# Longer weight runs with a new DMA model in the planner, a gain folded into weights, and three small steps moved to ScalarE in a decoder step on eight cores

## The chip, the cores and the metric

The kernel runs as one program on the 8 cores of one Trainium2 chip, each core on its own share of the batch. The time is device microseconds (us) of the slowest core. A program on all eight cores has a second, slower state in some executions: one die of four cores, or both, then shows a lower granted TensorE clock and the time is some per cent longer.

In the profile PE is TensorE, PEld its weight load, DVE VectorE, ACT ScalarE, POOL GpSimd and SP SyncE. A line such as `AR<-w_out` names the destination and the source of an operation. `pb` is a bank of PSUM and `AR` is the large working area in SBUF. Nearly every operation is emitted by one helper, so all carry the line number L252 and are told apart by their tiles and shapes. In the code cuts `ts`, `tt`, `stt`, `scan`, `act` and `cp` are helpers that record one elementwise operation each, and `dma` records a load. `...` marks what is left out, and comments are mine.

## The reference, cut to what matters

The step is one decoder layer for 2048 prompt tokens and 128 sample tokens per core. A mixer (one input projection, two head groups, one output projection) is followed by a squared-ReLU MLP and by a gated per-layer embedding.

```python
z = rmsnorm(h, norm_mix) @ w_in
u, vg, q, k, vm, o, zi, zf = jnp.split(z, SPLITS, axis=-1)
u  = gelu(u);  vg = layernorm(gelu(vg), gm_ln_g, gm_ln_b)         # head group A
y_gm = _gmlp_mix(u, vg, gm_ws, gm_bs, gm_len)
ig = zi + ml_b_i;  lf = log_sigmoid(zf + ml_b_f)                  # the gate rows, head group B
hm, state = _mlstm(q, k, vm, ig, lf, state, ml_len)
hm = rmsnorm(hm.reshape(B, T, ML_HEADS, ML_HEAD_DIM), ml_norm)    # the gain that is folded
y_ml = sigmoid(o) * hm
h = h + concat([y_gm, y_ml]) @ w_out
h = h + square(relu(rmsnorm(h, norm_ffn) @ w_up)) @ w_down        # the MLP
...                                                               # gated embedding, final norm
```

The tiles of 128 tokens are worked off in two passes: 8 prompt tiles and the sample tile first, then the other 8 prompt tiles. Each pass is a mixer and then an MLP. The weights are loaded again in the second pass.

Of the kernel before, what the change touches and what calls it, by code (L numbers as in the profile page):

```python
# [312 lines left out]
class Op:  # L313
    __slots__ = ("eng", "dma", "calls", "reads", "writes", "cost", "nbytes", "idx", "rank", "preds", "succs", "npred",
                 "pts", "tset", "fin", "tready", "after", "tok", "tag", "__dict__")
# [9 lines left out]
class Plan:  # L325
# [66 lines left out]
    def schedule(self, caps):  # L392
# [28 lines left out]
        while len(order) < n:  # L421
# [48 lines left out]
            if o.dma:  # L470
                free[e] = s + o.cost
                d0 = max(free[e] + 1.0, dma_free)
                dma_free = d0 + o.nbytes / 290e3
                o.fin = dma_free + 1.2
            else:
                o.fin = free[e] = s + o.cost
                if e == "act" and o.tset is not None:
                    tabs = (SETS[o.tset] & tabs) or SETS[o.tset]
# [32 lines left out]
def build():  # L511
# [27 lines left out]
    P = Plan()  # L539
    from contextlib import ExitStack  # L540
    with ExitStack() as st:
# [78 lines left out]
        def dma(out, in_, eng="sp", after=(), **kw):  # L620
            nb = 4 * _nelem(out) * list(out.ap)[0][1]
            return P.add(eng, (out, in_, kw), [in_], [out], 0.9 if eng == "pool" else 0.06, dma=True, nbytes=nb,
                         after=after)
# [87 lines left out]
        WIN = [WA.bf(8 * 512, k8(8)) for _ in range(6)]  # L711
# [7 lines left out]
        COLS = dict(u=0, v=512, q=1024, k=1536, m=2048, o=2560)  # L719
        WSLOT = dict(u=0, v=1, o=2, q=3, k=4, m=5)  # L720
        WORDER = ("u", "v", "o", "q", "k", "m")
# [57 lines left out]
        def load_win(names, **kw):  # L779
            v = w_in.rearrange("(k p) n -> p k n", p=128)  # L780
            for nm in names:
                dma(WIN[WSLOT[nm]], v[:, :, COLS[nm]:COLS[nm] + 512], eng="pool", **kw)
# [7 lines left out]
        load_win("u")  # L790
# [72 lines left out]
        def stage_P(grp):  # L863
# [6 lines left out]
            def feat(nm, fin):  # L870
                w = WIN[WSLOT[nm]]
                for hp in range(2):
                    p = ps("P")
                    for hh in range(2):
                        h = hp * 2 + hh
                        mm(p[:, hh * n:(hh + 1) * n],
                           [(w[:, kc, h * 128:(h + 1) * 128], at[:, kc, 0:n]) for kc in range(8)])
                    fin(p[:, 0:2 * n].rearrange("p (h t) -> p h t", h=2), slice(hp * 2, hp * 2 + 2))

            def tokm(nm, j):  # L880
                w = WIN[WSLOT[nm]]
                p = ps("P")
                mm(p, [(at[:, kc, j * 128:(j + 1) * 128], w[:, kc, :]) for kc in range(8)])
                return p
# [3 lines left out]
            for j, t in enumerate(grp):  # L888
                vn = VN[t["n"] % 2]
                act(vn, tokm("v", j), AF.Gelu_apprx_tanh)  # L890
                st6, mv, tm, rs = small(t["n"], 4, 6), small(t["n"], 10, 2), small(t["n"], 12, 1), small(t["n"], 13, 1)
                dve("bn_stats", st6, vn)
                dve("bn_aggr", mv, st6)
                rstd(rs, tm, mv[:, 1:2], 1.0, EPS)
                ts("dve", vn, vn, mv[:, 0:1], ALU.subtract, rs, ALU.mult)
                tt("pool", XH[t["n"] % 3], vn, GROW[:], ALU.mult)
                if t["ty"] == 1 or t["i"] == NPT - 1:
                    brow = SQ.rearrange("p h t -> p (h t)")
                    dma(brow, lnb.partition_broadcast(128), after=marks)
                    tt("pool", vn, vn, GROW[:], ALU.mult)  # L900
                    tt("pool", vn, vn, brow, ALU.add)
                    dma(o_Vs if t["ty"] == 1 else o_Vp, vn)
# [3 lines left out]
            for h in range(4):  # L906
                ts("dve", SGT[d2][:, h, 0:n], SGT[d2][:, h, 0:n], 1.0, ALU.add, GN[:, G_MLG + h:G_MLG + h + 1], ALU.mult)
            feat("q", lambda p, hs: cp("act", QT[d2][:, hs, 0:n], p))
            feat("k", lambda p, hs: act(KT[d2][:, hs, 0:n], p, AF.Copy, scale=QK_SCALE))
            for j, t in enumerate(grp):  # L910
                cp("act", VAUG[t["n"] % 4][:, :, 0:128], tokm("m", j).rearrange("p (h d) -> p h d", h=4))
            return pg, marks

        def stage_G(grp, pg):
# [11 lines left out]
            ts("dve", aa, pg[0:4, 0:n], GBI[0:4, 0:1], ALU.add)  # L926
# [28 lines left out]
            ts("dve", r3[0:4, 0:n], RR, -1.0, ALU.mult)  # L955
# [45 lines left out]
        def stage_M(grp, gs):  # L1001
# [3 lines left out]
            for j, t in enumerate(grp):  # L1005
# [80 lines left out]
                tt("dve", yt[:, 4:8, :], py[:, 0:512].rearrange("p (h t) -> p h t", h=4), SGT[d2][:, :, tk], ALU.mult)  # L1086
# [27 lines left out]
        def load_q(qd):  # L1114
            wu, wd = WU[qd % 2], WD[qd % 2]
            w_up_v = w_up.rearrange("(k p) n -> p k n", p=128)
            for hf in range(2):
                c0 = qd * 1024 + hf * 512
                dma(wu[:, :, hf * 512:(hf + 1) * 512], w_up_v[:, :, c0:c0 + 512], eng="pool")
# [55 lines left out]
        for si, sg in enumerate(SGS):  # L1175
# [3 lines left out]
            if si > 0:  # L1179
                load_win("uvoq")  # L1180
                P.tag = "vaug"
                for v_ in VAUG:
                    memset("pool", v_[:, :, 128:129], 1.0)
            for gi_, grp in enumerate(groups):
# [8 lines left out]
                if si == 0 and gi_ == 0:  # L1193
                    load_win("v", after=nops[:1])
# [4 lines left out]
                    load_win("o", after=nops[1:])  # L1199
                    nops = stage_N(groups[1], 1)  # L1200
                    load_win("qkm", after=nops)
                    dma(WOUT, w_out.rearrange("(k p) n -> p k n", p=128), eng="pool", after=nops)
                elif gi_ == 0:
                    load_win("km")
                    dma(WOUT, w_out.rearrange("(k p) n -> p k n", p=128), eng="pool")
# [139 lines left out]
```

## The kernel before: the parts that the change and the argument touch

The code that builds the kernel records all operations with what they depend on, and a **planner** then puts them into one fixed order for each engine. On the chip each engine works through its own list in that order. The planner is a list scheduler: again and again it takes the operation that can start first by its own cost model. Ties within 0.02 us go to the one written earlier.

```python
CROSS, SAME = 0.22, 0.06
TABLE = 1.3                                   # us, charged for a ScalarE function-table load
# Plan.schedule, shortened
for o in ready[e]:
    s = max(free[e], o.tready)
    if e == "pe":
        ...                                   # PSUM banks
    elif e == "act" and o.tset is not None and not (SETS[o.tset] & tabs):
        s += TABLE                            # Exp, Ln, Tanh, Gelu; a copy (Copy, Identity) has no tset
    cand.append((s, o))
s0 = min(c[0] for c in cand) + 0.02
best[e] = min((c for c in cand if c[0] <= s0), key=lambda c: c[1].rank)
...
if o.dma:                                     # the model of DMA: one queue, in order, 290 bytes per ns
    free[e] = s + o.cost
    d0 = max(free[e] + 1.0, dma_free)
    dma_free = d0 + o.nbytes / 290e3
    o.fin = dma_free + 1.2
```

What must stay in order comes from `_link`. For a PSUM tile, uses by the same engine form a run without order inside it, and a run waits for all of the run before it. So two reads of one PSUM tile by **different** engines are ordered, and two reads by the **same** engine are not.

```python
if r and r[-1][0] == o.eng and r[-1][1] == w and (o.eng == "pe" or not w):
    r[-1][2].append(o.idx)                    # same engine, same kind: joins the run
else:
    r.append((o.eng, w, [o.idx]))
if len(r) > 1:
    P.update(r[-2][2])                        # the whole run before must be done
```

The loads at the start and the steps that the change moves:

```python
def load_win(names, **kw):                    # six blocks of 512 columns of w_in, 2 KB runs, on POOL's queue
    v = w_in.rearrange("(k p) n -> p k n", p=128)
    for nm in names:
        dma(WIN[WSLOT[nm]], v[:, :, COLS[nm]:COLS[nm] + 512], eng="pool", **kw)

def consts_b(af):                             # issued after all weights of the mixer, w_out last
    dma(OH[:], coh, eng="pool", after=af)     # one-hot table: brings the gate rows to all partitions by matmul
    dma(MSK[:], cmask, after=af)              # no eng: SyncE's queue
    ...

# stage_P
ts("dve", vn, vn, mv[:, 0:1], ALU.subtract, rs, ALU.mult)                    # layernorm scaling
...
for h in range(4):                            # (1 + tanh) * gain, the gain of ml_norm
    ts("dve", SGT[d2][:, h, 0:n], SGT[d2][:, h, 0:n], 1.0, ALU.add, GN[:, G_MLG + h:G_MLG + h + 1], ALU.mult)

# stage_G: pg is one PSUM tile with both gate rows
act(L, pg[32:36, 0:n], AF.Exp, bias=GBI[32:36, 1:2], scale=-1.0)             # ScalarE
act(L, L, AF.Ln, bias=1.0)                                                   # ScalarE
ts("dve", aa, pg[0:4, 0:n], GBI[0:4, 0:1], ALU.add)                          # VectorE
scan(NB, L, ZROW[0:4, 0:n], 0.0, ALU.add, ALU.max)                           # VectorE, needs Ln
...
ts("dve", r3[0:4, 0:n], RR, -1.0, ALU.mult)

# stage_M
mmx([(pc[:, h, :], OH[:, h, :], r3[:, tk], True, True) for h in range(4)])   # "the OH matmul", first of them at 90 us
...
tt("dve", yt[:, 4:8, :], py[...], SGT[d2][:, :, tk], ALU.mult)               # gating
```

## Time and profile before

| | before |
|---|---|
| time, median of the three runs before the change | 1023.42 us (1022.73 to 1027.23) |
| TensorE busy on the slowest core | 895.8 of 1020.3 us (88%) |
| VectorE, ScalarE busy | 581.2 us, 391.8 us |
| first OH matmul starts | 90.8 us |
| software DMA queue (POOL's), share of 16 engines | 40.9% |

The page of the kernel before starts with busy time by engine. Its second part cuts the span into 40 slices of about 25.5 us, with one digit each for the busy tenths; PEclk is the granted TensorE clock in tenths.

```profile
PE 895.8 (88%) x5807; PEld 539.0 (53%) x5875; DVE 581.2 (57%) x1118; ACT 391.8 (38%) x711; POOL 264.4 (26%) x370
...
PE   2578898937999999999997678998899999999994
PEclk9798899967999999999999889999999999999997
```

TensorE is the bound, and its row of digits says where it is not full: the first three slices, slice 9 with a 3 (the sample tile), and slices 22 to 25 with 6 to 8 (the turn to the second pass). The view of waits names what TensorE waited for (total us, times, longest). Here `sC` is the state of the samples, `pp` and `psm` are the embedding inputs of the prompt and the samples, and `wgate` (tile WGT) holds the weights of the gate rows. The two longest entries, waits for ScalarE (31.8) and VectorE (29.6), are left out in this cut:

```profile
...
PE pb L252 <- DMA AR<-sC: 15.7, 1, 15.7
PE pb L252 <- DMA AR<-w_in: 10.7, 2, 6.7
...
PE pb L252 <- DMA AR<-pp: 3.6, 1, 3.6
```

OH is the last load that POOL issues at the start (its next one follows at 53.9 us), as the timeline (start, length, engine) and then the DMA view (KB each, us from issue to landing) show:

```profile
27.14 0.90 POOL L276 DMA_DIRECT2D AR<-w_out  x1
28.00 0.59 POOL L276 DMA_DIRECT2D OH<-coh  x1
...
90.83 0.61 PE L252 MATMUL pb<-R_0,OH 128*128 128x128 bf16 x8
```

```profile
OH<-coh POOLq DMA_DIRECT2D x1, 128.0 KB, 59.0
```

A load of 128 KB took 59 us to land, because it stood behind megabytes of weights on the same queue. The first OH matmul comes 4 us after the landing. The windows view (busy us and count for each engine in each stretch, then clock and DMA share) shows stretches at work:

```profile
core 2: us, PE busy (x) PEld busy (x) DVE busy (x) ACT busy (x) POOL busy (x), PEclk, DMA share, GB/s
60.00:80.00 20.00, 14.64 (x116) 10.70 (x114) 9.66 (x24) 8.46 (x17) 4.50 (x5) 0.91 1.10 179
640.00:660.00 20.00, 18.23 (x147) 11.84 (x150) 18.36 (x42) 12.19 (x21) 10.18 (x14) 1.00 0.00 1
660.00:680.00 20.00, 19.74 (x162) 14.69 (x163) 18.07 (x46) 12.06 (x22) 7.16 (x9) 1.00 0.00 1
```

In the second mixer (640 to 680 us) TensorE and VectorE are both nearly full.

The groups that the change means to remove or alter (busy us and mean ns, then idle before them):

```profile
L252 DVE TENSOR_SCALAR AR<-AR,GN 128x256 bf16<-128x256 bf16 x32 | 12.6, 434 | 9.9 <-ACT AR L252 9.7
...
L252 DVE TENSOR_SCALAR AR<-AR,SMALL 128x512 f32<-128x512 f32 x17 | 10.6, 626 | 6.6 <-POOL SMALL L252 6.4
...
L252 DVE TENSOR_TENSOR AR<-pb,AR 128x512 bf16<-128x512 bf16 x17 | 7.0, 414 | 0.1
```

These are the gate gain, the layernorm scaling and the gating.

### The profile page before, as it was taken

The numbers are of one execution on the slowest core, as the hardware profiler recorded it, in microseconds if no ns is written. First come the engines' busy times: TensorE is split into PE (matmuls) and PEld (weight loads), VectorE is DVE, ScalarE is ACT, GpSimd is POOL, SyncE is SP. The second block draws the span as 40 slices with busy tenths as digits, with TensorE's granted clock in tenths as the row PEclk, the third lists the DMA queues.
The fourth block names the chain that finished last, engine by engine and source line by source line (L and its number), as shares of the span: only waits on it lengthen the run. The fifth ranks groups of instructions, "written<-read, shape, count | busy, mean of one in ns | idle before, by whom it ended". The sixth has DMA issues, their size and how long they took to land.

```text
span 1020.3 us, 17111 instructions; the slowest of 8 cores (1003.6 to 1020.3 us)
## 1 busy us (share of the span) xinstructions
PE 895.8 (88%) x5807; PEld 539.0 (53%) x5875; DVE 581.2 (57%) x1118; ACT 391.8 (38%) x711; POOL 264.4 (26%) x370
## 2 busy tenths in 40 slices
PE   2578898937999999999997678998899999999994
PEld 2465476624455555555553267576656555565542
DVE  2354878445656774444665537988864444445664
ACT  4245356425311121114544547655532112124543
POOL 3233345443202220011232323545520001001211
PEclk9798899967999999999999889999999999999997
DMA  9993010996677768065249400003999909000111
GB/s 166 183 172 45 12 45 6 109 146 97 104 142 136 177 161 133 1 86 88 86 105 203 121 22 2 1 2 51 138 144 162 161 2 155 11 1 4 68 45 62
DMA packets 80689, 90.59 MB, mean 89 GB/s; under 512 B 13656, under 2 KB 62044, under 8 KB 80604
## 3 DMA queue, kind: packets, MB, share of 16 engines
q0 software_dynamic: 54224, 59.18, 40.9%
q1 hardware_dynamic: 26380, 30.32, 9.8%
q8 instruction: 48, 0.79, 0.3%
q14 instruction: 37, 0.30, 0.1%
HBM read 134.74 MB, written 13.93 MB: 146 GB/s over the span
## 4 chain that ended last, share of the span: by engine, by line
PE 75%; DMA 9%; DVE 6%; issue 5%; ACT 3%; POOL 2%; DVEq 0%; SPq 0%; POOLq 0%; ACTq 0%
PE pb L252 75%; DVE AR L252 3%; DMA AR<-sC 3%; DMA AR<-w_in 3%; DMA AR<-pp 2%; ACT AR L252 2%; POOL SMALL L252 1%; DMA H<-xp 1%; DVE H L252 1%; DVE SMALL L252 1%; DVE ROWX L252 1%; ACT L252 1%; POOL AR L252 0%; DVE ROWR L252 0%; POOL CST L252 0%
## 5 line engine op out<-in xcount | busy, mean ns | idle before, releaser
L252 PE MATMUL pb<-AR 128*128 128x512 bf16 (+4 forms) x4856 | 838.0, 331 | 62.3 <-DVE AR L252 20.9
L252 PEld LDWEIGHTS pb<-AR 128*128 128x128 bf16 x4924 | 470.8, 100 | 393.8 <-issue 86.3
L252 ACT ACTIVATE AR<-pb 128x384 f32<-128x384 f32 (+5 forms) x349 | 175.5, 513 | 476.0 <-PE pb L252 387.7
L252 DVE TENSOR_TENSOR H<-H,pb 128x512 f32<-128x512 f32 x170 | 116.4, 685 | 136.5 <-PE pb L252 136.3
L252 DVE TENSOR_TENSOR AR<-AR 128x384 bf16<-128x384 f32 (+2 forms) x209 | 122.8, 589 | 109.1 <-ACT AR L252 108.3
L252 ACT ACTIVATE AR<-H 128x1024 bf16<-128x1024 f32 x68 | 71.7, 1054 | 54.4 <-PE pb L252 26.9
L252 PE MATMUL pb<-IDB,AR 128*128 128x128 bf16 x578 | 53.5, 237 | 42.6 <-ACT AR L252 28.7
L252 POOL TENSOR_SCALAR SMALL<-SMALL 128x1 f32<-128x1 f32 x85 | 26.3, 310 | 245.4 <-ACT AR L252 201.9
L252 DVE TENSOR_TENSOR AR<-pb,GN 128x1024 bf16<-128x1024 bf16 x51 | 61.6, 1218 | 36.4 <-PE pb L252 36.4
L252 POOL TENSOR_TENSOR SMALL<-SMALL,NEGH 128x1 f32<-128x1 f32 (+1 forms) x102 | 69.3, 681 | 49.8 <-DVE SMALL L252 29.6
L252 PEld LDWEIGHTS pb<-IDB,AR 128*128 128x128 bf16 x578 | 43.0, 107 | 57.7 <-issue 48.9
L252 ACT ACTIVATE AR<-H,SMALL 128x1024 bf16<-128x1024 f32 x51 | 58.1, 1145 | 35.3 <-POOL SMALL L252 34.9
L276 POOL DMA_DIRECT2D AR<-w_up x16 | 15.0, 935 | 132.7 <-PE pb L252 132.3
L252 DVE TENSOR_TENSOR AR<-pb,AR 128x512 f32<-128x512 f32 (+3 forms) x86 | 43.7, 523 | 9.4 <-ACT AR L252 8.4
L252 ACT ACT_TABLE_LOAD x29 | 37.2, 1283 | 16.1 <-PE pb L252 10.2
L252 DVE SCALAR_TENSOR_TENSOR AR<-AR,pb 128x512 f32<-128x512 f32 x34 | 23.2, 684 | 29.6 <-PE pb L252 20.8
L252 ACT ACTIVATE AR<-AR 128x512 f32<-128x512 f32 x34 | 21.3, 629 | 23.8 <-DVE AR L252 17.2
L252 POOL TENSOR_TENSOR AR<-AR,GROW 128x512 bf16<-128x512 f32 (+1 forms) x19 | 25.5, 1341 | 16.5 <-PE pb L252 8.5
L276 POOL DMA_DIRECT2D AR<-w_in x12 | 11.0, 920 | 68.3 <-PE pb L252 64.3
L252 DVE SCALAR_TENSOR_TENSOR AR<-H,SMALL,AR 128x1024 f32<-128x1024 f32 x17 | 22.9, 1346 | 9.1 <-POOL SMALL L252 8.7
L252 ACT ACTIVATE AR<-pb,GSM 128x129 f32<-128x129 f32 x68 | 20.7, 366 | 13.7 <-PE pb L252 13.5
L276 POOL DMA_DIRECT2D AR<-w_down x16 | 12.2, 765 | 51.4 <-PE pb L252 51.3
(101 smaller groups left out, 434.7 us busy)
## 6 DMA issues: line engine op xcount, KB each, us to landing
AR<-w_up POOLq DMA_DIRECT2D x16, 1024.0 KB, 16.0
AR<-w_down POOLq DMA_DIRECT2D x16, 1024.0 KB, 18.9
AR<-w_in POOLq DMA_DIRECT2D x12, 1024.0 KB, 17.5
H<-xp SPq DMA_DIRECT2D x16, 512.0 KB, 4.6
y_p<-AR SPq DMA_DIRECT2D x16, 512.0 KB, 2.9
AR<-w_out POOLq DMA_DIRECT2D x2, 2048.0 KB, 41.8
AR<-sC SPq DMA_DIRECT2D x8, 512.0 KB, 5.0
AR<-w_pg POOLq DMA_DIRECT2D x2, 2048.0 KB, 27.4
```

Source lines behind the costliest of these rows:

```text
L252: ins = getattr(e, name)(**kw)
L276: lambda e, out=out, in_=in_, sem=sem, kw=kw: e.dma_start(out=out, in_=in_, **kw).then_inc(sem, 16))
```

## The change

The intent has three parts. Weights are to be read in runs of 4 KB instead of 2 KB, for fewer and larger packets. The gain of ml_norm is to be multiplied once into the rows of w_out, and no longer into each tile's gate. Work is to move from VectorE (57% busy) to ScalarE (38%). With the first part comes a new model of DMA in the planner.

```diff
             if o.dma:
                 free[e] = s + o.cost
-                d0 = max(free[e] + 1.0, dma_free)
-                dma_free = d0 + o.nbytes / 290e3
-                o.fin = dma_free + 1.2
+                took = o.nbytes / o.rate
+                if o.nbytes < 2e6:                        # "small" loads do not queue
+                    o.fin = free[e] + 2.2 + took * (2 if dma_free > free[e] + 1 else 1)
+                    dma_free = max(dma_free, free[e] + 1) + took
+                else:
+                    dma_free = max(free[e] + 1.5, dma_free) + took
+                    o.fin = dma_free + 1.2
...
+            o.rate = (320e3 if run >= 4096 else 265e3 if run >= 2048 else 180e3) * (1.0 if eng == "pool" else 1.1)
...
-        WIN = [WA.bf(8 * 512, k8(8)) for _ in range(6)]
+        WPAIR = [WA.bf(8 * 1024, k8(8)) for _ in range(3)]   # u|v, m|o, q|k
...
+        def load_wout(af):
+            dma(WOUT, w_out.rearrange("(k p) n -> p k n", p=128), eng="pool", after=af)
+            for h in range(4):
+                ts("dve", WOUT[:, 4 + h, :], WOUT[:, 4 + h, :], GN[:, G_MLG + h:G_MLG + h + 1], ALU.mult)
...
-                ts("dve", vn, vn, mv[:, 0:1], ALU.subtract, rs, ALU.mult)
+                nm = small(t["n"], 14, 1)
+                stt("dve", nm, mv[:, 0:1], -1.0, rs, ALU.mult, ALU.mult)
+                act(vn, vn, AF.Identity, bias=nm, scale=rs)
...
-            for h in range(4):
-                ts("dve", SGT[d2][:, h, 0:n], SGT[d2][:, h, 0:n], 1.0, ALU.add, GN[...], ALU.mult)
...                                                          # m is now projected before q and k
-            ts("dve", aa, pg[0:4, 0:n], GBI[0:4, 0:1], ALU.add)
+            act(aa, pg[0:4, 0:n], AF.Identity, bias=GBI[0:4, 0:1])
...
-            ts("dve", r3[0:4, 0:n], RR, -1.0, ALU.mult)
+            act(r3[0:4, 0:n], RR, AF.Copy, scale=-1.0)
...
-                tt("dve", yt[:, 4:8, :], py[...], SGT[d2][:, :, tk], ALU.mult)
+                stt("dve", yt[:, 4:8, :], SGT[d2][:, :, tk], 1.0, py[...], ALU.add, ALU.mult)
...
-            for hf in range(2):                              # w_up: two loads of 512 columns
-                dma(wu[:, :, hf * 512:(hf + 1) * 512], w_up_v[:, :, c0:c0 + 512], eng="pool")
+            dma(wu, w_up_v[:, :, qd * 1024:(qd + 1) * 1024], eng="pool")
...
-                load_win("uvoq")
+                load_win(["uv", "mo"])
...
-                    load_win("qkm", after=nops)
-                    dma(WOUT, ..., eng="pool", after=nops)
+                    load_win(["qk"], after=nops)
+                    load_wout(nops)
```

At the start u and v are still loaded one by one, and o, m, q, k in pairs.

More of the change, by code (lines that the diff above doesn't have):

```diff
@@ L314 @@
     __slots__ = ("eng", "dma", "calls", "reads", "writes", "cost", "nbytes", "idx", "rank", "preds", "succs", "npred",
-                 "pts", "tset", "fin", "tready", "after", "tok", "tag", "__dict__")
+                 "pts", "tset", "fin", "tready", "after", "tok", "tag", "rate", "__dict__")
 SETS = {"gelu": frozenset(("g",)), "tanh": frozenset(("g", "e")), "exp": frozenset(("e", "l")),
@@ L621, in dma @@
             nb = 4 * _nelem(out) * list(out.ap)[0][1]
-            return P.add(eng, (out, in_, kw), [in_], [out], 0.9 if eng == "pool" else 0.06, dma=True, nbytes=nb,
-                         after=after)
+            run = min(list(out.ap)[-1][1], list(in_.ap)[-1][1]) * 4
+            o = P.add(eng, (out, in_, kw), [in_], [out], 0.9 if eng == "pool" else 0.06, dma=True, nbytes=nb,
+                      after=after)
+            o.rate = (320e3 if run >= 4096 else 265e3 if run >= 2048 else 180e3) * (1.0 if eng == "pool" else 1.1)
+            return o
         def mmx(items):
@@ L718, in build, with win @@
         WD[1] = WB.bf(8 * 1024, k8(8))
-        COLS = dict(u=0, v=512, q=1024, k=1536, m=2048, o=2560)
-        WSLOT = dict(u=0, v=1, o=2, q=3, k=4, m=5)
-        WORDER = ("u", "v", "o", "q", "k", "m")
+        COLS = dict(u=0, v=512, q=1024, k=1536, m=2048, o=2560, uv=0, qk=1024, mo=2048)
+        WLOC = dict(u=(0, 0), v=(0, 512), m=(1, 0), o=(1, 512), q=(2, 0), k=(2, 512), uv=(0, 0), mo=(1, 0), qk=(2, 0))
+        def win(nm):
+            i_, o_ = WLOC[nm]
+            return WPAIR[i_][:, :, o_:o_ + 512 * len(nm)]
         AB = [LOW.bf(DM) for _ in range(2)]
@@ L781, in load_win @@
             for nm in names:
-                dma(WIN[WSLOT[nm]], v[:, :, COLS[nm]:COLS[nm] + 512], eng="pool", **kw)
+                dma(win(nm), v[:, :, COLS[nm]:COLS[nm] + 512 * len(nm)], eng="pool", **kw)
+        def load_wout(af):
+            dma(WOUT, w_out.rearrange("(k p) n -> p k n", p=128), eng="pool", after=af)
+            for h in range(4):
+                ts("dve", WOUT[:, 4 + h, :], WOUT[:, 4 + h, :], GN[:, G_MLG + h:G_MLG + h + 1], ALU.mult)
         P.tag = "start"
@@ L789, in build @@
         memset("pool", NEGH[:], -0.5)
-        load_win("u")
+        load_win(["u"])
         cp("dve", IDB[:], IDF[:])
@@ L870, in feat @@
             def feat(nm, fin):
-                w = WIN[WSLOT[nm]]
+                w = win(nm)
                 for hp in range(2):
@@ L880, in tokm @@
             def tokm(nm, j):
-                w = WIN[WSLOT[nm]]
+                w = win(nm)
                 p = ps("P")
@@ L905, in stage_P @@
             feat("o", lambda p, hs: act(SGT[d2][:, hs, 0:n], p, AF.Tanh, scale=0.5))
-            for h in range(4):
-                ts("dve", SGT[d2][:, h, 0:n], SGT[d2][:, h, 0:n], 1.0, ALU.add, GN[:, G_MLG + h:G_MLG + h + 1], ALU.mult)
+            for j, t in enumerate(grp):
+                cp("act", VAUG[t["n"] % 4][:, :, 0:128], tokm("m", j).rearrange("p (h d) -> p h d", h=4))
             feat("q", lambda p, hs: cp("act", QT[d2][:, hs, 0:n], p))
             feat("k", lambda p, hs: act(KT[d2][:, hs, 0:n], p, AF.Copy, scale=QK_SCALE))
-            for j, t in enumerate(grp):
-                cp("act", VAUG[t["n"] % 4][:, :, 0:128], tokm("m", j).rearrange("p (h d) -> p h d", h=4))
             return pg, marks
@@ L1085, in stage_M @@
                 trs([(py[:, h * 128:(h + 1) * 128], yml[:, h, :], IDB[:]) for h in range(4)])
-                tt("dve", yt[:, 4:8, :], py[:, 0:512].rearrange("p (h t) -> p h t", h=4), SGT[d2][:, :, tk], ALU.mult)
+                stt("dve", yt[:, 4:8, :], SGT[d2][:, :, tk], 1.0, py[:, 0:512].rearrange("p (h t) -> p h t", h=4),
+                    ALU.add, ALU.mult)
                 for nn in range(2):
@@ L1116, in load_q @@
             w_up_v = w_up.rearrange("(k p) n -> p k n", p=128)
-            for hf in range(2):
-                c0 = qd * 1024 + hf * 512
-                dma(wu[:, :, hf * 512:(hf + 1) * 512], w_up_v[:, :, c0:c0 + 512], eng="pool")
+            dma(wu, w_up_v[:, :, qd * 1024:(qd + 1) * 1024], eng="pool")
             for hf in range(2):
@@ L1193, in build @@
                 if si == 0 and gi_ == 0:
-                    load_win("v", after=nops[:1])
+                    load_win(["v"], after=nops[:1])
                     for t in groups[1]:
@@ L1198, in build @@
                     dma(WGT[:], wgate.rearrange("(k p) n -> p k n", p=128), eng="pool", after=nops[1:])
-                    load_win("o", after=nops[1:])
+                    load_win(["mo"], after=nops[1:])
                     nops = stage_N(groups[1], 1)
-                    load_win("qkm", after=nops)
-                    dma(WOUT, w_out.rearrange("(k p) n -> p k n", p=128), eng="pool", after=nops)
+                    load_win(["qk"], after=nops)
+                    load_wout(nops)
                 elif gi_ == 0:
-                    load_win("km")
-                    dma(WOUT, w_out.rearrange("(k p) n -> p k n", p=128), eng="pool")
+                    load_win(["qk"])
+                    load_wout(())
                 P.tag = f"A{si}P{gi_}"
```

## The prediction

> What bounds the kernel now. The page gives TensorE 88% busy (896 of 1020 us), VectorE 57%, ScalarE 38%. In the windows view the two MLP stretches are saturated (262-530 us: 265 of 268 busy; 740-980 likewise). The ~124 idle us of TensorE sit in six places: the start, 0-87 us (53 busy of 87); the first mixer part, 87-190 (90 of 103); the sample tile, 190-219 (13 of 29, one wait of 15.7 us for the state load AR<-sC); 219-262 (32 of 43); the turn from the first pass to the second, 530-600 (50 of 70, with a 3.6 us wait for AR<-pp); the second mixer part, 600-740 (128 of 140); and the tail.
>
> DMA. Start: the 16 DMA engines are above 100% busy from 20 to 80 us. The POOL queue delivers in order u, v, wgate, o, q, k, m, w_out and last the one-hot table OH, which lands at 87 us; the first OH matmul starts at 90.8. Packets of 1024 B (a 2 KB run cast to bf16) take 98 ns median, 117 mean; 2048 B packets (w_down, w_out, 4 KB runs) 173 median, 200-210 mean: 11-15% less per byte. The Trainium skill, "DMA: Bandwidth & Descriptors", section "Why small descriptors are slow (HBM only)", names a fixed cost per packet; these two durations agree. Over the kernel 26,600 packets of 1024 B become 13,300 of 2048 B: about 33 us of 16-engine time, software queue 40.9% to about 38%. On the critical path lie only: m,o,q,k before OH, 4 x 1024 x (118-105 ns)/16 = 3-5 us; w_up ahead of sC, about 2 us; k,m ahead of pp at the turn, 2-3 us. Against it: o waits for its whole 4 MB pair (one block is 7.7 us); and the w_up load waits for both u and v to be free (2.7 us later here). The planner no longer queues small loads behind large ones, although sC and pp really waited 23-28 us; it may place their matmuls too early.
>
> VectorE. Removed, by groups: gate gain TENSOR_SCALAR 15.1 us, layernorm scale 10.6, gate rows aa and r3 6.7. Added, estimated: nm 17 x 0.17 = 2.9, w_out scaling 8 x 0.42 = 3.3, and the gating op, 0.41 us as a TENSOR_TENSOR in bf16, as SCALAR_TENSOR_TENSOR probably 0.68 (the rate that op shows here): +4.6. Net about -21 (581 to 560). ScalarE gains 17 x 0.63 + 18 x 0.42 = +18 (392 to 410). VectorE is near full only at 100-120 and 620-680 us (18 of 20): I expect 2-5 us of TensorE idle back in the mixer parts; aa and r3 on ScalarE lengthen the gate chain by two engine crossings.
>
> Sum: start -4, sample tile and turn -3, mixer -4, order changes +-6: about 1012 us. Interval 998 to 1023. Chances: faster by over 2% 0.16, within 2% 0.82, slower 0.02.
>
> Right if: queue near 38%; OH lands near 82-84 us; VectorE falls by about 20 us, ScalarE rises by about 18, table loads stay at 29 or fewer; TensorE's busy time is unchanged and idle falls by about 11 us, mostly before 90 us and in the mixer parts.
>
> Wrong if: the static order moves sC or pp matmuls so that these waits grow (slower), or the sC wait or the turn, 16 and 20 idle us, largely vanishes by a better order (faster); if HBM, shared by cores, not packet cost, limits the start, 4 KB runs bring nothing.

## More of the kernel before

TensorE works 14.6 of 20 us while it has no OH.

The timeline of the first gate rows of the second pass:

```profile
601.38 1.28 ACT L252 ACT_TABLE_LOAD   x1 [0.26 <-PE pb L252]
602.68 0.47 ACT L252 ACTIVATE ROWL<-pb,GBI 4x256 f32<-4x256 f32 x1
603.25 0.47 DVE L252 TENSOR_SCALAR ROWX<-pb,GBI 4x256 f32<-4x256 f32 x1 [1.05 <-ACT ROWL L252]
...
619.23 1.28 ACT L252 ACT_TABLE_LOAD   x1
620.52 0.41 ACT L252 ACTIVATE ROWL<-ROWL 4x256 f32<-4x256 f32 x1
...
621.04 0.68 DVE L252 TENSOR_TENSOR_SCAN ROWN<-ROWL,ZROW 4x256 f32<-4x256 f32 x1 [3.94 <-ACT ROWL L252]
```

The first ACTIVATE is Exp, the second is Ln, ROWX is the row `aa`, and the scan can start 18.4 us after Exp. Note the releaser of `aa`: it waited for ScalarE's Exp, although it does not need its result. That is the order edge of `_link`.

## The result, and the profile after

| | before | after |
|---|---|---|
| median of 4 fast runs | 1024.8 us (1022.73 to 1027.23) | 1069.66 us (1066.66 to 1071.08) |
| ratio, with 95% interval | | 1.0433 (1.0397 to 1.0469) |
| TensorE busy / idle on the slowest core | 895.8 / 124.5 us | 901.7 / 166.6 us |
| VectorE, ScalarE busy | 581.2, 391.8 us | 564.5, 406.8 us |
| mean granted clock, die medians | 0.956, 0.957 | 0.936, 0.938 |

The kernel became 4.3% slower, where about 1012 us (998 to 1023) had been predicted. A ratio in this document is the mean time of one kernel's fast runs over that of the other's fast runs of the same rounds, so it is not quite the ratio of the medians quoted beside it. Results were correct in every run.

The engines did about what was predicted of them: VectorE fell by 16.7 us and ScalarE rose by 15.0. The loss is TensorE's idle time, and the page shows it mainly in two places. (The trace of the slowest core before lacks 68 of the 5875 matmuls, so its busy time is read a little low.)

```profile
PE 901.7 (84%) x5875; PEld 539.6 (51%) x5875; DVE 564.5 (53%) x1072; ACT 406.8 (38%) x743; POOL 253.5 (24%) x357
...
PE   3503999867979899999996789789699999999994
PEclk9756999998989999999998889899889999999997
```

The third slice (53 to 80 us) went from 7 to 0. And slices 26 and 27 (about 670 to 720 us, in the second mixer) are 7 and 8, where the kernel before has two 9s. TensorE's waits:

```profile
PE pb L252 <- DMA OH<-coh: 36.3, 1, 36.3
...
PE pb L252 <- DMA WGT<-wgate: 14.8, 1, 14.8
PE pb L252 <- DMA AR<-sC: 11.0, 3, 4.9
PE pb L252 <- DMA AR<-psm: 10.6, 1, 10.6
```

The waits for OH, wgate and psm did not exist before, and all are for small loads; the one for sC did. Over the eight cores the wait for OH is 28.3 to 36.3 us, with a median of 31.3. Did OH land later? Timeline and DMA view:

```profile
25.50 0.88 POOL L276 DMA_DIRECT2D AR<-w_out  x1
26.37 0.57 POOL L276 DMA_DIRECT2D OH<-coh  x1
...
91.47 0.58 PE L252 MATMUL pb<-R_0,OH 128*128 128x128 bf16 x4 [36.34 <-DMA OH<-coh]
```

```profile
OH<-coh POOLq DMA_DIRECT2D x1, 128.0 KB, 65.0
```

It landed at about the same moment (26.37 + 65.0 = 91.4 on this core; the medians over the cores are 86.2 us before and 86.5 after). What differs is what stands in front of the OH matmul in TensorE's list: 406 matmuls before, 142 after. TensorE came to it at 55 us, and with a fixed list it cannot pass it. The windows view shows the empty stretch, and then the second loss:

```profile
core 3: us, PE busy (x) PEld busy (x) DVE busy (x) ACT busy (x) POOL busy (x), PEclk, DMA share, GB/s
60.00:80.00 20.00, 0.00 (x0) 0.00 (x0) 1.02 (x4) 0.00 (x0) 1.46 (x4) 0.50 1.05 169
620.00:640.00 20.00, 19.44 (x150) 15.35 (x151) 3.42 (x8) 11.22 (x18) 5.46 (x10) 0.92 0.01 2
640.00:660.00 20.00, 20.00 (x165) 14.94 (x163) 4.83 (x10) 11.88 (x18) 5.25 (x8) 1.00 0.01 2
660.00:680.00 20.00, 14.22 (x112) 10.33 (x111) 11.15 (x24) 14.39 (x26) 4.79 (x7) 0.95 0.00 1
...
700.00:720.00 20.00, 17.32 (x152) 12.44 (x151) 19.41 (x44) 11.34 (x25) 10.37 (x14) 1.00 0.00 1
```

From 60 to 80 us TensorE does not run at all and its clock is 0.50. The Trainium skill, "TensorE: Matmul & The Clock Gate", section "What's actually happening", has an idle state of 1.2 GHz out of 2.4; the 0.50 agrees. In the second mixer (620 to 660 us) VectorE has work for 3.4 and 4.8 of 20 us while TensorE is full; then, at 700 to 720, VectorE is full (19.4) and TensorE is not (17.3). The two no longer overlap. The timeline of the first gate rows there:

```profile
628.28 0.47 ACT L252 ACTIVATE ROWX<-pb,GBI 4x256 f32<-4x256 f32 x1 [0.28 <-PE pb L252]
...
633.50 0.60 ACT L252 ACTIVATE AR<-pb 128x512 bf16<-128x512 f32 x1 [1.13 <-PE pb L252]
635.25 0.60 ACT L252 ACTIVATE AR<-pb 128x512 bf16<-128x512 f32 x1 [1.15 <-PE pb L252]
...
650.23 1.28 ACT L252 ACT_TABLE_LOAD   x1
651.53 0.47 ACT L252 ACTIVATE ROWL<-pb,GBI 4x256 f32<-4x256 f32 x1
...
668.65 1.28 ACT L252 ACT_TABLE_LOAD   x1
669.95 0.42 ACT L252 ACTIVATE ROWL<-ROWL 4x256 f32<-4x256 f32 x1
...
670.47 0.68 DVE L252 TENSOR_TENSOR_SCAN ROWN<-ROWL,ZROW 4x256 f32<-4x256 f32 x1 [3.97 <-ACT ROWL L252]
```

`aa` (ROWX) is now first. Exp follows 23 us later and not 1 us earlier, and the scan starts 42.2 us after `aa`, where it started 18.4 us after Exp before. In between ScalarE copies PSUM tiles: 0.60 us of work and 1.15 us of idle time, over and over.

The groups that changed. The new gating takes 679 ns where the old one took 414, the layernorm takes 809 ns on ScalarE, and w_out is scaled in 8 operations:

```profile
L252 DVE SCALAR_TENSOR_TENSOR AR<-AR,pb 128x512 bf16<-128x512 bf16 x17 | 11.5, 679 | 0.3 <-PE pb L252 0.2
...
L252 ACT ACTIVATE AR<-AR,SMALL 128x512 f32<-128x512 f32 x17 | 13.7, 809 | 3.2 <-DVE SMALL L252 3.0
...
L252 DVE TENSOR_SCALAR AR<-AR,GN 128x1024 bf16<-128x1024 bf16 x8 | 3.7, 507 | 0.0
```

**Where the time went.** The MLP matmuls have 384 columns, so the last one of each MLP marks the end of a pass in the timeline. Each pass is cut in two at its first MLP matmul; the table gives the sum of the two parts' medians over the eight cores of the profiled run, in us:

| | first pass | of it TensorE idle | second pass | of it TensorE idle | rest |
|---|---|---|---|---|---|
| before | 521.4 | 67.7 | 416.1 | 28.3 | 71.8 |
| after | 549.0 | 100.0 | 436.4 | 44.2 | 72.3 |
| difference | +27.6 | +32.3 | +20.3 | +15.9 | +0.5 |

So there are two losses of similar size, one in each pass.

### The profile page after: what moved, and what is told of

It is laid out like the page before. It is cut to its first block, busy times and chain, and to the rows that moved or that the text cites. A ratio compares the mean times of both kernels' runs of the same rounds, so it can differ in the third digit from the quotient of the medians.

```text
span 1068.3 us, 17120 instructions; the slowest of 8 cores (1045.8 to 1068.3 us)
## 1 busy us (share of the span) xinstructions
PE 901.7 (84%) x5875; PEld 539.6 (51%) x5875; DVE 564.5 (53%) x1072; ACT 406.8 (38%) x743; POOL 253.5 (24%) x357
## 3 DMA queue, kind: packets, MB, share of 16 engines
q0 software_dynamic: 40704, 59.18, 39.1%
## 4 chain that ended last, share of the span: by engine, by line
PE 67%; DMA 14%; DVE 5%; issue 5%; another core or an unknown queue 3%; ACT 3%; POOL 2%; SPq 0%; POOLq 0%; DVEq 0%; ACTq 0%
PE pb L252 67%; DMA AR<-sC 7%; DVE AR L252 2%; DMA AR<-psm 2%; DMA WGT<-wgate 2%; ACT AR L252 2%; POOL SMALL L252 1%; DMA o_Cs<-AR 1%; DMA H<-xp 1%; DMA AR<-lnb 1%; DVE SMALL L252 1%; DVE ROWX L252 1%; DVE H L252 0%; ACT L252 0%
## 5 line engine op out<-in xcount | busy, mean ns | idle before, releaser
L252 PE MATMUL pb<-AR 128*128 128x256 bf16 (+4 forms) x4924 | 844.7, 332 | 47.0 <-DVE AR L252 27.8
L252 DVE TENSOR_TENSOR AR<-AR 128x384 bf16<-128x384 f32 (+2 forms) x209 | 120.2, 578 | 99.3 <-ACT AR L252 98.6
L252 PEld LDWEIGHTS pb<-IDB,AR 128*128 128x128 bf16 x578 | 42.2, 105 | 54.8 <-issue 45.8
L252 DVE SCALAR_TENSOR_TENSOR AR<-AR,pb 128x512 f32<-128x512 f32 (+1 forms) x51 | 34.6, 682 | 36.9 <-PE pb L252 21.1
L276 POOL DMA_DIRECT2D AR<-w_up x8 | 7.5, 943 | 158.5 <-PE pb L252 154.8
L252 DVE TENSOR_TENSOR AR<-pb,AR 128x258 f32<-128x258 f32 (+2 forms) x69 | 36.9, 552 | 10.3 <-PE pb L252 7.3
L252 ACT ACT_TABLE_LOAD x26 | 33.4, 1283 | 9.2 <-DMA H<-xp 5.5
L252 PE MATMUL pb<-R_0,OH 128*128 128x128 bf16 x40 | 4.3, 236 | 37.6 <-DMA OH<-coh 36.3
L252 DVE SCALAR_TENSOR_TENSOR AR<-AR,DECBS,pb 128x129 f32<-128x129 f32 x64 | 17.6, 342 | 23.6 <-DMA AR<-sC 22.7
L252 ACT ACTIVATE AR<-AR 128x512 f32<-128x512 f32 x34 | 21.2, 628 | 16.6 <-DVE AR L252 13.7
L252 ACT ACTIVATE AR<-pb,GSM 128x129 f32<-128x129 f32 x68 | 20.4, 368 | 17.0 <-PE pb L252 16.7
```

Of the source, the lines that this page charges most:

```text
L252: ins = getattr(e, name)(**kw)
L276: lambda e, out=out, in_=in_, sem=sem, kw=kw: e.dma_start(out=out, in_=in_, **kw).then_inc(sem, 16))
```

## The experiments

**Theory 1 (first pass).** The new model of DMA causes it. It lets any load under 2 MB land soon after its issue, whatever stands in its queue. From the code, OH is taken to land some 5 us after issue (an estimate from the formula: 262,144 source bytes at 180 bytes per ns are 1.5 us, twice, plus 2.2); it took 65.0. So the planner puts the OH matmul much too early. The rival: the load order, the pairs and the operations of the kernel itself do it, and the old planner would have waited as well.

**Theory 2 (second pass).** The rival reasons were the same DMA model, or slower steps on ScalarE. The theory was this one: `aa` on ScalarE has lost the edge that put it after Exp. A copy to `aa` needs no table and Exp is charged 1.3 us for one, so the greedy planner takes `aa` first, and after it every PSUM copy that can start within 1.3 us (they come every 1.75 us, with 1.15 us idle). Exp is put off until no copy is at hand. Where `aa` does not go first, Exp is not caught in this: in the trace after the change `aa` ends at 628.75 us, so an Exp could start 1.3 us later, at 630.05 (an estimate), and the next copy starts at 630.02, just ahead of it. Without the 0.47 us of `aa` in front, Exp could start at 629.58 and be first.

All runs side by side, columns as above, with the time of the whole and its ratio to the kernel before. "Rule" says whether small loads jump the queue in the planner; `aa` says which engine copies it.

| run | rule | aa | first pass | second pass | median us | ratio (95%) |
|---|---|---|---|---|---|---|
| before | no | VectorE | 521.4 | 416.1 | 1024.8 | 1 |
| after | yes | ScalarE | 549.0 | 436.4 | 1069.66 | 1.0433 (1.0397 to 1.0469) |
| e1_old_planner | no | ScalarE | 526.9 | 437.6 | 1044.65 | 1.0237 (1.0194 to 1.0280) |
| e2_planner_only | yes | VectorE | 550.9 | 420.2 | 1058.97 | 1.0362 (1.0311 to 1.0413) |
| e3_pool_fifo | SyncE only | ScalarE | 542.5 | 435.7 | 1057.54 | 1.0382 (1.0331 to 1.0434) |
| e4_oh_early | yes | ScalarE | 525.9 | 435.5 | 1047.04 | 1.0258 (1.0219 to 1.0297) |
| e5_aa_back | no | VectorE | 512.8 | 420.8 | 1015.57 | 0.9916 (0.9882 to 0.9949) |
| e6_aa_only | no | ScalarE | 520.4 | 438.8 | 1044.50 | 1.0200 (1.0157 to 1.0242) |
| e7_no_act_moves | no | VectorE | 524.7 | 418.6 | 1034.87 | 1.0055 (0.9984 to 1.0125) |
| x_e3_aa_back (profile slow) | SyncE only | VectorE | 529.0 | 418.5 | 1030.67 | 1.0006 (0.9972 to 1.0040) |
| e8_exp_first | no | ScalarE, after Exp | 526.4 | 423.5 | 1034.30 | 1.0094 (1.0043 to 1.0145) |
| e9_after_aa_back | yes | VectorE | 577.8 | 417.2 | 1075.79 | 1.0498 (1.0444 to 1.0552) |
| x10_best_oh | no | VectorE | 504.8 | 420.6 | 1004.41 | 0.9794 (0.9748 to 0.9840) |
| x11_first_oh | no | ScalarE, after Exp | 509.4 | 423.7 | see text | none |
| e13_rates_only | no | ScalarE | 529.9 | 435.0 | 1041.23 | 1.0151 (1.0126 to 1.0176) |
| e14_before_oh | no | VectorE | 534.6 | 416.8 | 1032.68 | 1.0060 (1.0028 to 1.0092) |

The medians take all runs, slow ones too (several kernels had one). The kernel before had medians of 1020.62, 1020.86, 1024.67 and 1025.38 us.

### e1_old_planner: the whole change but for the planner's model

```diff
-                took = o.nbytes / o.rate
-                if o.nbytes < 2e6: ...
+                d0 = max(free[e] + 1.0, dma_free)
+                dma_free = d0 + o.nbytes / 290e3
+                o.fin = dma_free + 1.2
```

> The kernel after, with the old planning model of DMA (one queue, 290 bytes per ns) put back; all operations, tiles and loads stay as after. Its TensorE order has 386 matmuls before the first OH matmul, as before (406), where after has 142. Theory (the loss is the order made by the new planning model): 1005 to 1025 us, the OH wait of 36 us and the wgate wait of 15 us nearly gone. Rival (the paired 4 MB loads, or the moved vector work, cost the time): 1050 to 1075 us.

Measured 1044.65 us, 1.0237. The OH matmul stands after 386 others again and the wait is gone; the first pass fell from 549.0 to 526.9 us. But the second pass stayed at 437.6. The expected time was missed: theory 1 explains one loss, and a second one has another cause.

### e2_planner_only: the kernel before with the new model alone

```diff
-                d0 = max(free[e] + 1.0, dma_free) ...
+                took = o.nbytes / o.rate ...          # and o.rate in dma()
```

> The kernel before, with only the new planning model of DMA; operations, tiles and loads as before. 158 matmuls stand before the first OH matmul. Theory (planning model): 1055 to 1080 us, with a wait for OH of 30 us or more. Rival (paired loads or moved vector work): 1015 to 1035 us.

Measured 1.0362, as expected; the wait for OH, 27.2 us on the slowest core, is a little under the 30 us expected. Not one operation differs from the kernel before, only the order, and the first pass is 550.9 us, as long as after the change (549.0). The OH matmul stands after 158 others. This run and e1 show theory 1 from both sides: the model alone makes the first loss, and without the model all but 5.5 us of it is gone (521.4 to 526.9).

### e3_pool_fifo: small loads queue on POOL, and not on SyncE

```diff
-                if o.nbytes < 2e6:
+                if o.nbytes < 2e6 and e != "pool":
```

> The kernel after, one line of the planning model changed: the rule for loads under 2 MB (they overtake what is queued) no longer holds for loads issued by POOL, which queue in order; the new rates stay. 398 matmuls stand before the first OH matmul. Theory (that one rule, on the POOL queue, is what hurt): 1000 to 1025 us. Rival inside the theory (the new rates, or the same rule for SyncE loads, hurt): above 1035 us.

A miss, 1.0382. The OH matmul moved back to 398 matmuls, and the time until the first MLP matmul fell from 248.8 to 223.7 us. But the MLP part of the pass grew from 300.1 to 318.8. TensorE's idle time there rose from 11.5 to 24.7 us, of which 9.0 (median) is a wait for `sC` loads on POOL's queue and 13.6 are waits for VectorE (none and 10.5 after the change); the other 5.5 us of the growth are TensorE's work that now falls behind the first MLP matmul. In the same part VectorE waits 22.6 us for `sC` loads on SyncE's queue, which the model still takes to be quick. That wait is not what grew, for the kernel after has it too (22.7 us on its slowest core). It goes with the rule: in the median over the cores the six kernels that let SyncE's small loads jump the queue have 15 to 23 us of it, and none of the other ten has more than 1.2. The two loads that it waits for longest took 21.0 and 14.7 us, so they are not quick: the Trainium skill, "DMA: Bandwidth & Descriptors", section "Queues, rings and completion order", says that each DMA engine serves the queues it has work for in turn. That a small SyncE load still suffers beside POOL's full queue shows in the DMA view of before: 10.1 us for MSK (128 KB), 13.7 for SBC (256 KB), against 59 for OH, which is on POOL's queue itself. So in-order queueing of POOL alone is not a good model.

### e4_oh_early: OH loaded right after the first weight block

```diff
         load_win(["u"])
+        dma(OH[:], coh, eng="pool")
...
-            dma(OH[:], coh, eng="pool", after=af)
```

> The kernel after with the new planning model, but the OH load issued on the POOL queue right behind the first weight block instead of behind w_out, so that it lands by about 25 us. The order still has OH matmuls early (150 before the first). Theory: the 36 us wait for OH goes, part of it comes back as waits for o, q, k or w_out, which land when they did: 1035 to 1055 us. Rival (the OH wait only covers time that the load of the weights would cost anyway): 1060 to 1072 us, with an equally long wait for w_in or w_out in its place.

Measured 1.0258, as expected. OH lands at 16.8 us (median), and the first pass is 525.9 us with the new model in place. This shows that the OH wait was real: of 31.3 us (median) 23.1 are won back. The timeline shows the next wait behind it:

```profile
79.34 0.26 DVE L252 CAST AR<-NCOLS 128x8 bf16<-128x8 f32 x2 [20.87 <-DMA NCOLS<-snT]
...
81.39 0.58 PE L252 MATMUL pb<-R,OH 128*128 128x128 bf16 x4 [18.58 <-DVE AR L252]
```

VectorE stands for 20.9 us before a cast that needs the 32 KB load `snT`, placed too early by the same rule, and TensorE waits 18.6 us for VectorE. When one load is mended, the planner's error shows at the next.

### e5_aa_back: e1, and `aa` back on VectorE

```diff
-            act(aa, pg[0:4, 0:n], AF.Identity, bias=GBI[0:4, 0:1])
+            ts("dve", aa, pg[0:4, 0:n], GBI[0:4, 0:1], ALU.add)
```

> The kernel of run e1 (after, with the old planning model), with one operation more undone: the gate row aa is copied out of PSUM by VectorE again, not by ScalarE. Theory (aa on ScalarE lets the planner take it at once and leave the Exp, which costs a table load, behind the PSUM copies; the gate chain of the second pass then starts 15 to 25 us late): the second mixer part falls back by 10 us or more, 1015 to 1032 us. Rival (the loss of e1 in the second pass is from the paired loads, the w_out scaling or the other moves to ScalarE): 1038 to 1050 us, like e1.

Measured 0.9916, as expected: with the new model and the move of `aa` taken out, what is left of the change is a gain of 0.8%. The second pass fell from 437.6 to 420.8 us. The first pass fell too, from 526.9 to 512.8, which I did not expect and cannot explain from one operation of 0.47 us.

### e6_aa_only: the kernel before, with only `aa` moved to ScalarE

```diff
-            ts("dve", aa, pg[0:4, 0:n], GBI[0:4, 0:1], ALU.add)
+            act(aa, pg[0:4, 0:n], AF.Identity, bias=GBI[0:4, 0:1])
```

> The kernel before with nothing changed but aa, copied by ScalarE. The ScalarE order then has 16 and 10 activations between the first aa of the second pass, its Exp and its Ln, where before has 12 from Exp to Ln. Theory: 1032 to 1048 us. Rival: 1018 to 1028 us, no change.

Measured 1.0200, as expected. One line costs 2%, all of it in the second pass: 416.1 to 438.8 us. In ScalarE's list the first Exp of the second pass moved from 341st to 362nd activation, behind `aa` at 346.

### e7_no_act_moves: e1, with `aa`, `r3` and the layernorm back on VectorE

```diff
-                nm = ...;  stt("dve", nm, ...);  act(vn, vn, AF.Identity, bias=nm, scale=rs)
+                ts("dve", vn, vn, mv[:, 0:1], ALU.subtract, rs, ALU.mult)
...
-            act(aa, ...);  act(r3[0:4, 0:n], RR, AF.Copy, scale=-1.0)
+            ts("dve", aa, ...);  ts("dve", r3[0:4, 0:n], RR, -1.0, ALU.mult)
```

> The old planning model, all three moves to ScalarE undone (aa, negated RR, layernorm scaling on VectorE); what is left of the change is the paired loads of w_in and w_up, m before q and k, and the gain folded into w_out. Theory: this part is worth a little, 1010 to 1024 us, as the prediction's DMA terms said. Rival (the paired loads delay o and w_up, and cost more than the faster packets give): 1028 to 1045 us.

Fast runs give 1.0055 (0.9984 to 1.0125); six runs scattered from 1019.56 to 1095.50 us, slow ones among them. The three fast ones (1019.56, 1028.00 and 1034.57) lie across both expected ranges, so this run decides nothing about its theory. The layernorm and `r3` on ScalarE would then be worth about 1.4% (1.0055 against e5's 0.9916), all of it in the first pass (524.7 against 512.8). That is no more than the scatter between orders that other runs show there, and TensorE of e7 waits 10.8 us (median) for `sC` in the MLP part, where e5 does not. So it is not shown that the two steps are worth this.

### x_e3_aa_back: e3, and `aa` back on VectorE

> A candidate that should beat both: after, with loads issued by POOL queued in order in the planning model (as in run e3), the new rates kept, and aa back on VectorE. Theory (the two causes add): 1005 to 1025 us, against 1057 for e3. Rival (e3 was slow for its rates or something else in the first pass): 1035 to 1050 us.

The edit is that of e5 on top of e3. The fast runs, 1021.34 and 1023.53 us, lie in the expected range, but with 1.0006 (0.9972 to 1.0040) the kernel does not beat the one before, as was hoped. The profiled run was slow, so its first pass of 529.0 us is not used (its undisturbed die has 530); its second pass, 418.5, is on the same side as all others with `aa` on VectorE.

### e8_exp_first: e1, `aa` on ScalarE, with the lost edge put back

```diff
-            act(L, pg[32:36, 0:n], AF.Exp, bias=GBI[32:36, 1:2], scale=-1.0)
+            ex_ = act(L, pg[32:36, 0:n], AF.Exp, bias=GBI[32:36, 1:2], scale=-1.0)
             act(L, L, AF.Ln, bias=1.0)
-            act(aa, pg[0:4, 0:n], AF.Identity, bias=GBI[0:4, 0:1])
+            aa_ = act(aa, pg[0:4, 0:n], AF.Identity, bias=GBI[0:4, 0:1])
+            aa_.preds.add(ex_.idx)
```

> Run e1 (after, old planning model, 1.024 of before) with aa still on ScalarE but one edge more in the plan: aa may not be taken before the Exp of the same gate rows. No operation is added, removed or moved. In the ScalarE order the distance from the first gate row to the Ln in the second pass falls from 28 activations to 14. Theory (the loss was the deferred Exp, not the 0.47 us that ScalarE spends on aa): 1010 to 1026 us, like e5 (0.992). Rival (ScalarE time or the extra engine crossing): 1036 to 1050 us, like e1.

This run tells "ScalarE is slower at it" from "the order is worse". `aa` stays on ScalarE and only its order edge to Exp returns. The timeline of the same gate rows:

```profile
612.99 1.28 ACT L252 ACT_TABLE_LOAD   x1 [0.26 <-PE pb L252]
614.28 0.47 ACT L252 ACTIVATE ROWL<-pb,GBI 4x256 f32<-4x256 f32 x1
615.40 0.46 ACT L252 ACTIVATE ROWX<-pb,GBI 4x256 f32<-4x256 f32 x1
...
632.95 0.68 DVE L252 TENSOR_TENSOR_SCAN ROWN<-ROWL,ZROW 4x256 f32<-4x256 f32 x1 [3.38 <-ACT ROWL L252]
```

From Exp to the scan it is 18.7 us, as before the change (18.4). The second pass is 423.5 us: of the 16.8 us between e1 and e5 the edge brings 14.1. The whole, 1034.30 us or 1.0094, missed the expected range of 1010 to 1026, since the first pass stayed near e1's (526.4 against 526.9). So the loss in the second pass is the order, and not the speed of ScalarE.

### e9_after_aa_back: the change as it was, with only `aa` back

> After with only aa back on VectorE, the new planning model kept: the fourth corner of the square of two causes (e5 0.992, e1 1.024, after 1.043). Theory, causes add: 1.008 to 1.020 of before, 1030 to 1043 us, with the waits for OH and wgate of the kernel after still there (109 matmuls before the first OH). Rival (they overlap: with the gate chain in time the planning model costs nothing, or with it late aa costs nothing): below 1020 or above 1060 us.

A miss: 1.0498. The edit is that of e5 on the changed kernel. The second pass did what theory 2 says, 436.4 to 417.2 us. But the first pass grew from 549.0 to 577.8. OH is not why, although its matmul now stands after 109 others and not 142: up to the first MLP matmul the pass takes 249.3 us against 248.8. All of the growth is in the MLP part, 300.1 to 328.5, where TensorE's idle time rose from 11.5 to 33.5 us; 14.7 of these (median) are a wait for `sC` on POOL's queue, which after the change was not in this part. With the new rule in place a small edit moved the pass by 29 us. The total even lies in the range given for the rival (above 1060), but not for its reason, an overlap of the two causes: undoing one of them made the loss from the other larger.

### x10_best_oh: e5, with OH early

```diff
+        dma(OH[:], coh, eng="pool")               # after load_win(["u"])
-            dma(OH[:], coh, eng="pool", after=af)
```

> A candidate to beat both: e5 (old planning model, aa on VectorE) with OH loaded right behind the first weight block. First OH matmul after 149 matmuls instead of 402, its load long landed. Hope: the first tiles of the first pass start their state part earlier, 995 to 1012 us. If the start is bound by the weight loads alone: 1010 to 1020 us, like e5.

Measured 1004.41 us (1002.30 to 1005.27), 0.9794: faster than both kernels, by 2.1% than before, and by some 6% than after (1004.41 against 1069.66 us, taken in different calls). The first pass is 504.8 us, with 59.4 us of TensorE idle time instead of 67.7 before. TensorE's row of the page's 40 slices:

```profile
PE   2668999688999999999995699999799999999994
```

The third slice is 6, and from slice 24 to 28 (576 to 701 us) TensorE shows 9 throughout; slice 29 is a 7.

### x11_first_oh: e8, with OH early

> The same with aa on ScalarE after its Exp (e8) and OH early. If e8 repairs the order: 995 to 1020 us; if not, above 1030 us.

Two of its four runs were slow (1127.10 and 1076.37 us), the two fast ones 1010.48 and 1010.93, in the expected range, and no interval is given. Its second pass is 423.7 us, like e8's; its first pass is 509.4 where e8 had 526.4.

### e13_rates_only: the change, with the rule off and the new rates kept

```diff
-                if o.nbytes < 2e6:
+                if False:
```

> After with the rule for loads under 2 MB taken out of the planning model for every queue (all loads queue), its new rates kept; aa still on ScalarE. Open after e3, which took the rule away for POOL alone: the first mixer part was repaired, the first MLP stretch was not (319 us against 295, with VectorE waiting 21 us for sC loads issued by SyncE). Theory (the rule also misjudges SyncE loads): the first pass takes 520 to 532 us as in e1 (527), the whole 1035 to 1050 us, 1.02 of before. Rival (the new rates did it): the first pass 540 us or more, the whole above 1050 us.

Measured 1.0151, as expected: the first pass is 529.9 us, close to e1's 526.9. It is the rule that small loads do not queue that did the damage, and not the rates.

### e14_before_oh: the kernel before, with OH early

> Before with only OH loaded right behind the first weight block. Tells how much of the candidate x10 (0.979 of before) is the early OH and how much the change itself. If OH: 0.983 to 0.993 of before; if the gain needs the change too: 0.995 to 1.005.

A miss: 1.0060 (1.0028 to 1.0092), slightly slower, with 534.6 us in the first pass. The edit is that of x10 on the kernel before. An early OH is no gain by itself; with e5's order it brought 8 us in the first pass and with e8's 17, and with the old order it cost 13. I have no explanation of that beyond the order.

### What is shown and what stays open

The second pass sorts all sixteen kernels cleanly: `aa` on VectorE 416 to 421 us, `aa` on ScalarE 435 to 439, `aa` on ScalarE behind Exp 423.5 and 423.7. Three pairs that differ in this line alone give 22.7 (before and e6), 16.8 (e5 and e1) and 19.2 us (e9 and after). That cause is shown. That the planner prefers the copies because of the 1.3 us it charges for the table is read from its code and fits the trace, where copies come at 1.15 us of idle time; no run changed that number by itself.

In the first pass, the rule with OH late gives 549.0, 550.9 and 577.8 us, and 542.5 with the rule on SyncE alone; queueing for all gives 504.8 to 534.6. The rule is shown as the cause of the loss: with OH late, the time up to the first MLP matmul, where OH is needed, is 242.9 to 249.3 us with the rule and 217.3 to 234.3 with queueing for all. What stays open is the scatter inside each class, some 30 us between orders whose operations hardly differ.

## Why the prediction was wrong, point by point

**The step that failed** is the term "order changes +-6". The prediction named the danger ("The planner no longer queues small loads behind large ones, although sC and pp really waited 23-28 us; it may place their matmuls too early") and gave it no size of its own. I looked at the two waits that already existed, sC and pp, and on TensorE these did not grow (medians over the cores: sC 11.1 to 10.2 us, pp 2.3 to 1.0). The one that mattered was OH, which before had *no* wait. The wait grew from nothing to 36.3 us (median 31.3) because the 264 matmuls that had hidden it were moved behind it. The prediction even noted that OH is last in its queue and lands at 87 us; it did not ask where the new model would think it lands. Measured size of the term: +22 us (e1 to after) to +30 us (before to e2).

**A second step failed with it**: "aa and r3 on ScalarE lengthen the gate chain by two engine crossings". The planner charges 0.22 us for a crossing. The runs showed in their place 17 to 23 us in the second pass, since moving `aa` took away an order edge, and Exp was put off behind copies.

**The other terms: near in sum, not shown one by one.** Without those two, the change measures 0.9916 of before, about 9 us at 1020 us, where the prediction's other terms sum to 11. Luck cannot be ruled out here. The gain is all in the first pass (521.4 to 512.8), whose length scatters by more than that between orders, and e1, which differs from e5 in `aa` alone, has no gain there (526.9); the second pass, where the turn and the mixer were to gain, is 4.7 us longer than before. What the prediction left out cost five times the sum.

**VectorE** was to fall by about 20 us and fell by 16.7; the gating op was predicted at 0.68 us and measures 679 ns. The scaling of w_out was undersized: 507 ns a piece against 420. **ScalarE** was to rise by 18 and rose by 15.0, with 26 table loads instead of 29. The layernorm was costed at 630 ns and takes 809. The Trainium skill, "ScalarE: Activation LUTs", section "What ACT_TABLE_LOAD costs", has 186 ns plus 0.833 ns per element plus about 93 ns for each operand that is a column of 128 values; with 512 elements and two such operands that is an estimate of 799 ns, so reading it would have been closer.

**OH's landing**, predicted at 82 to 84 us, is 86.5 after the change, and 83.2 to 84.2 in e1, e5, e7, e8 and e13, which keep the 4 KB runs with the queueing model. The longer runs thus helped there by the small amount predicted, and the new order gave it back: v was issued at 15.08 us instead of 10.77, because ScalarE now squared both x tiles first.

**The packets.** The software queue was to fall to about 38% and is 39.1% of a longer span. Packets of 1024 B went from 28,800 to 2,176, those of 2048 B from 12,800 to 26,112. The prediction had 33 us of 16-engine time saved; the median core shows 8 (422.7 to 414.6 us), and 19 in e5 (403.5). The Trainium skill, "DMA: Bandwidth & Descriptors", section "Why small descriptors are slow (HBM only)", names a fixed cost per packet, and the medians agree (98 ns for 1024 B, 173 for 2048 B). But the mean of the 2048 B packets was 217.6 ns after the change and 208.4 before. The saving was costed from means of before, as if they would stay. Whether more of such packets make each one slower is not shown: three kernels with 12,800 of them have means from 205 to 214 ns (before, e2, e6), and five with 26,112 from 212 to 224 (after, e1, e5, e7, e13). Little of this queue's time was on the critical path in any case: waits for w_in are 3% of the chain that the page before shows as ending last.

**The clock.** The mean granted clock fell from 0.956 to 0.936; on the slowest core after the change it was 0.50 for 37.5 us around the wait for OH, and 0.954 from 95 us on, where the slowest core before has 0.952. So the fall is a result of the wait, and not a separate cause.

## What to carry to other kernels

When a kernel's order is made by a planner, a change of its cost model is a change of the whole program: take the loads that now hide behind other work, ask when the new model believes they land, and compare that with the landing time in the trace. When an operation moves to another engine, ask not only what it costs there but which order edge the old placement gave for free, and who comes before whom on the new engine. Let a change of the model and a change of the operations be measured apart, for here a loss of 4.3% had two causes, one of each kind, and without them the change measured 0.8% faster.

## What the Trainium skill lacked or had wrong

- "ScalarE: Activation LUTs", section "What ACT_TABLE_LOAD costs", gives about 1283 ns for the load and a drain of about 1380 ns, 2.66 us in all for a switch. The load agrees (1.28 us), but no drain is seen in these traces: the next activation starts 1.30 us after the load's start (650.23 to 651.53 us after the change, 601.38 to 602.68 before), and after the change the load itself started 0.01 us after the activation in front of it had ended.
- "VectorE: DVE Perf Modes": its table of operations has tensor_tensor with a PSUM operand at the slowest tier. Here a TENSOR_TENSOR in bf16 with one operand in PSUM took 414 ns for 128x512, and 681 ns with a float32 operand. The page's section "Why PSUM operands drop a tier" does allow the middle tier for bf16, and the 414 ns agree with that section and not with the table.
- No page that I found gives a time for a scalar_tensor_tensor in bf16 with an operand in PSUM. For 128x512 in bf16 with one PSUM operand it took 679 ns, as long as in float32 (684), so replacing a bf16 tensor_tensor by it cost 265 ns each time.
- "DMA: Bandwidth & Descriptors" has no figure for how long a small load waits when queues are full. Here a 128 KB load behind the weights of its own queue landed after 59 to 65 us, and loads of 128 to 256 KB on the other queue after 10 to 14 us in the same stretch of the kernel before.
- The same page gives no time for a packet of 2048 B in a loaded kernel: here the median was 173 ns and the means, kernel by kernel, 205 to 224.
